# Split fp32r projections in the first mixer, one modulation moved to TensorE, dummy matmuls in the routing, and nineteen weight chunks loaded ahead

## The chip, the cores and the metric

One NeuronCore of a Trainium2 chip runs the whole kernel. The time is that of the device for one execution, in microseconds (us); the time shown for a kernel is the median of its runs. The profile is of one further execution, with its own time. The engines are TensorE (PE, matrix products), VectorE (DVE), ScalarE (ACT), GpSimd (POOL) and SyncE (SP), which here issues the transfers of the weights. PEld is TensorE's loading of the stationary operand. The granted clock of TensorE is given as a share of its full 2.4 GHz.

## The reference

A trunk of two layers over 256 tokens of width 1024. Each layer normalizes, scales and shifts its input by columns that are computed from a conditioning vector c (six modulations per layer: shift, scale and gate of the mixer, shift, scale and gate of the feed-forward part), runs a mixer, adds its gated output, and does the same with a feed-forward part. The part of the reference that the change touches:

```python
# layer 0, mixer: one input projection split into u, v (A) and p (B)
u, v = split(gelu(uv));  v = layernorm(v)
sv = einsum('gts,bnsgd->bntgd', tril(w_s), v) + b_s        # chunks of 128 tokens
a  = u * sv
pooled = trailing_mean(p, windows 2, 4, 8, 16) - p
b  = einsum('bsgd,gde->bsge', pooled, w_grp) * scale
x  = x + gate * (concat(a, b) @ w_out)

# layer 1, feed-forward: top 2 of 8 experts
logits = h @ router_w
top_v, top_i = top_k(logits, 2);  wts = softmax(top_v)
y = sum_e gates[..., e] * swiglu(h, w_gu[e], w_down[e])    # 8 experts, 1024 -> 3584 -> 1024
```

The ada modulations are `c_act @ ada_w + ada_b`, a matrix of 1024 x 6144 per layer. All weights are float32 in device memory, 466 MB that are read once.

## The kernel before, in words

The kernel streams the weights in chunks of 1 MB (128 partitions x 2048 float32) from SP's queue into a ring of buffers named `raw`: 5 at first, 8 more (`keep`) and 3 more (`extra`) when the dense part has ended. A list `order` says which chunk comes next; whenever a buffer is left (`leave`) the next load is issued.

Products of the dense part are made of fp32r matmuls: an operand x is split into a rounded part H and the remainder L, and x w is taken as xH wH + xL wH + xH wL, three matmuls. ACT makes H (line 121), DVE subtracts to get L (line 124). The first mixer is an exception: its projection of `vp` (v and p, line 649) and its `gate_u` (line 666) multiply in plain float32, where one matmul is executed as several passes and shows two records.

The first mixer: `normed` gives the normalized tokens; the class `HT` transposes them in quarters q = 0 to 3 on PE (`flip`, line 285) and evacuates each quarter with its scale and shift (`evac`, line 299 on DVE). The scale and shift of a quarter come from `ada(0, 1, q)` and `ada(0, 0, q)`, each two weighted sums over a chunk on DVE (line 568) and a bias (line 596). A modulation can be computed on PE instead, with `ada_rows`: 16 small row products (line 579), a copy of the row by ACT (line 585), and `turn`: four products with one column (line 589) and the bias on DVE (line 591). The loop over q runs in an order written out by hand: within `tc.manual_schedule` the instructions of an engine are kept in the order of the program text. What stands behind the closing of that order (`hand.close()`) is placed by a planner, which orders by estimated times, until the next hand-written part. After the loop come `gate_u(0)`, the gelu of v, its layernorm on DVE and POOL (lines 683 to 691), the pooling matrices (lines 704 to 713), `gate_u(1)`, the products with w_s (line 730), and the output projection with split operands (lines 316 to 322 and 356 to 359), followed by the flips and the feed-forward part of layer 0 from 106 us.

The routing of layer 1: `Close` finishes the residual of layer 1's mixer, the tokens are flipped (line 1300) and multiplied with the router (line 1314), `Route.top2` finds the two experts of each token (lines 427 to 436), `place` and `counts` count the tokens of each expert with small products (lines 441 to 449). An expert's tokens are collected with a 0/1 matrix P, which `Gather.rows` builds by comparing slots with a row of integers (`iota`, line 1388; Q on line 1390), and `pick64` multiplies with the tokens (line 1416); `part64` evacuates. Then `seq`, a list of chunk events, is run: per block four chunks of gate/up weights and two of down weights. Experts with up to 64 tokens (S) use plain float32 with the two halves of the array's columns (lines 1527 and 1547), experts with up to 128 (L) use the split. S and L blocks alternate with LEAD = 3 blocks of S ahead; FIRST = 16 is the number of chunks before the first L block, and up to so many chunks are loaded, as far as buffers are free (16), before the first event runs. The last expert ends with `scatter2_front` (line 1553) and the addition into the result.

## Time and profile before

| what | value |
|---|---|
| median of 3 runs | 1250.69 us (1250.29 to 1253.85) |
| profiled execution | 1250.61 us |
| its span, first to last instruction | 1248.6 us |
| mean granted clock of TensorE | 0.989 |
| PE / DVE / ACT / POOL busy | 1199.2 / 735.3 / 501.3 / 67.7 us |
| read from device memory | 465.76 MB, 374 GB/s over the span |

Share of the span by engine and by stage are read from different views: the page sums over everything, while windows of a few us show which engine is full in one stage. A busy PE is one with a matmul in flight; at half clock it is as busy as at full clock. A gap of PE has beside it the instruction that released it, in brackets in the timeline. Records of matmuls overlap, so their pitch is read from the starts.

### The profile page before, as it was taken

To read this page: it belongs to the slowest core of one execution; us is meant where nothing else is said; L and a number is where in the kernel's file an instruction comes from. 1 tells how busy PE (TensorE), PEld (TensorE's weight loads), DVE (VectorE), ACT (ScalarE), POOL (GpSimd) and SP (SyncE) were. 2 spreads that over 40 slices of the span, in tenths; PEclk is the share of its full clock that TensorE was granted. 3 is DMA by queue.
4 is the path that set the end of the run, shared out by engine and by line. 5 is a ranking of instruction groups with operands and counts; after the bars stand their busy time and mean duration, and the time that the engine had idled before them with its cause. 6 is when DMAs were issued, how large, how long until landed. Compare 5 with 4: busy or idle time off the path is not lost.

```text
span 1248.6 us, 18665 instructions
## 1 busy us (share of the span) xinstructions
PE 1199.2 (96%) x7255; PEld 866.1 (69%) x7255; DVE 735.3 (59%) x1098; ACT 501.3 (40%) x775; POOL 67.7 (5%) x105
## 2 busy tenths in 40 slices
PE   5999999999999899999999999999999999999997
PEld 2577999997987666666666676666675666666663
DVE  5797988886895355546264656263555652653531
ACT  2147443445763234444153344252433541433410
POOL 2810000001320000000000000000000000000000
PEclk9999999999999799999999999999999999999999
DMA  9898999984657899999999999999999999999995
GB/s 357 352 376 306 354 337 349 355 313 176 237 203 277 343 405 421 419 419 419 419 420 419 419 420 419 420 419 420 419 419 412 418 419 420 420 420 418 420 418 202
DMA packets 65904, 468.11 MB, mean 375 GB/s; under 512 B 7568, under 2 KB 7824, under 8 KB 9616
## 3 DMA queue, kind: packets, MB, share of 16 engines
q1 hardware_dynamic: 65520, 466.32, 92.5%
q8 instruction: 59, 0.97, 0.3%
q10 hardware_dynamic: 288, 0.52, 0.1%
q14 instruction: 37, 0.30, 0.1%
HBM read 465.76 MB, written 1.05 MB: 374 GB/s over the span
## 4 chain that ended last, share of the span: by engine, by line
PE 85%; DVE 7%; issue 2%; ACT 2%; POOL 1%; DMA 1%; SPq 0%; DVEq 0%; ACTq 0%; POOLq 0%
PE gu L1527 20%; PE o L1547 10%; PE o L316 3%; PE g L316 3%; PE pb L337 3%; PE g L318 3%; PE u L318 3%; PE o L318 3%; PE u L316 3%; PE o L322 3%; PE g L322 3%; PE pb L335 3%; PE u L322 3%; PE pb L334 3%; PE pa L649 2%
## 5 line engine op out<-in xcount | busy, mean ns | idle before, releaser
L121 ACT CAST H<-raw 128x1024 fp32r<-128x1024 f32 x350 | 344.2, 1047 | 34.2 <-PE pb L335 13.2
L147 DVE TENSOR_TENSOR raw<-raw,H 128x1024 fp32r<-128x1024 f32 x252 | 297.5, 1222 | 39.9 <-ACT H L121 22.6
L1527 PE MATMUL gu<-raw,hgS 128*64 128x256 f32 x2240 | 253.8, 383 | 0.0
L1527 PEld LDWEIGHTS gu<-raw,hgS 128*64 128x64 f32 x2240 | 157.4, 137 | 89.0 <-issue 13.8
L124 DVE TENSOR_TENSOR L<-raw,H 128x1024 fp32r<-128x1024 f32 (+1 forms) x98 | 118.2, 1219 | 26.6 <-PE pb L337 14.5
L1547 PE MATMUL o<-raw,aS 128*64 128x512 f32 x560 | 130.4, 599 | 0.0
L568 DVE SCALAR_TENSOR_TENSOR junk<-raw,cact 128x1024 bf16<-128x1024 f32 x88 | 108.8, 1259 | 8.4 <-DMA raw<-in_ada 8.2
L334 PE MATMUL pb<-hH,H 128*128 128x256 f32 x432 | 103.1, 279 | 0.0
L335 PE MATMUL pb<-hL,H 128*128 128x256 f32 x432 | 102.9, 279 | 0.0
L1533 DVE TENSOR_TENSOR msg<-msg,gu 128x256 f32<-128x256 f32 x35 | 14.7, 421 | 125.2 <-ACT msg L1532 125.1
L1547 PEld LDWEIGHTS o<-raw,aS 128*64 128x64 f32 x560 | 37.0, 137 | 64.3 <-issue 60.0
L334 PEld LDWEIGHTS pb<-hH,H 128*128 128x128 f32 x432 | 81.2, 188 | 0.4
L335 PEld LDWEIGHTS pb<-hL,H 128*128 128x128 f32 x432 | 81.1, 188 | 0.4
L1481 DVE TENSOR_TENSOR msg<-msg,u 128x512 f32<-128x512 f32 x21 | 14.4, 687 | 109.0 <-ACT msg L1480 109.0
L1532 ACT ACTIVATE msg<-gu 128x256 f32<-128x256 f32 x35 | 13.4, 384 | 161.3 <-PE gu L1527 161.2
L1480 ACT ACTIVATE msg<-g 128x512 f32<-128x512 f32 x21 | 12.5, 597 | 151.3 <-PE g L322 151.3
L316 PE MATMUL g<-H,hgH 128*128 128x512 f32 x168 | 67.3, 401 | 0.0
L322 PE MATMUL u<-raw,hgH 128*128 128x512 f32 x168 | 66.5, 396 | 0.0
L318 PE MATMUL g<-H,hgL 128*128 128x512 f32 x168 | 66.5, 396 | 0.0
L318 PE MATMUL u<-H,hgL 128*128 128x512 f32 x168 | 66.4, 395 | 0.0
L316 PE MATMUL u<-H,hgH 128*128 128x512 f32 x168 | 66.3, 395 | 0.0
L322 PE MATMUL g<-raw,hgH 128*128 128x512 f32 x168 | 66.3, 394 | 0.0
(391 smaller groups left out, 1631.4 us busy)
## 6 DMA issues: line engine op xcount, KB each, us to landing
raw<-in_mgu SPq DMA_DIRECT2D x224, 1024.0 KB, 16.0
raw<-in_mdn SPq DMA_DIRECT2D x112, 1024.0 KB, 15.3
raw<-in_ada SPq DMA_DIRECT2D x48, 1024.0 KB, 6.9
raw<-in_fgu SPq DMA_DIRECT2D x22, 1024.0 KB, 7.7
raw<-in_fdn SPq DMA_DIRECT2D x11, 1024.0 KB, 7.5
raw<-in_oin_c SPq DMA_DIRECT2D x6, 1024.0 KB, 5.3
raw<-in_ein_vp SPq DMA_DIRECT2D x4, 1024.0 KB, 9.3
raw<-in_eout SPq DMA_DIRECT2D x4, 1024.0 KB, 7.2
```

Of the source, the lines that this page charges most:

```text
L121: act.copy(self.to(q), raw[:, q * self.f:(q + 1) * self.f])
L124: eng.tensor_tensor(self.to(q), raw[:, q * self.f:(q + 1) * self.f], high.half(q).bitcast(F32), OP.subtract)
L147: vec.tensor_tensor(l[:, at], raw[:, at], h.half(q).bitcast(F32), OP.subtract)
L316: pe.matmul(o, xH(k, i), wH(k, n), start=first and m == 0, stop=False)
L318: pe.matmul(o, xL(k, i), wH(k, n), start=False, stop=False)
L322: pe.matmul(o, xH(k, i), wL(k, n), start=False, stop=last and m == len(ks) - 1)
L334: pe.matmul(o, wH(k), hH[:, k, :], start=(k == 0), stop=False)
L335: pe.matmul(o, wH(k), hL[:, k, :], start=False, stop=False)
L337: pe.matmul(o, wL(k), hH[:, k, :], start=False, stop=(k == KD - 1))
L568: vec.scalar_tensor_tensor(junk, raw[:, a * D:(a + 1) * D], 1.0, cact, OP.mult, OP.mult, accum_out=mods[:, l, j + a:j + a + 1])
L1527: pe.matmul(gu[HALF[h], n * 256:(n + 1) * 256], g_.full[:, k, :], w[:, lo:lo + 256], start=(k == 0 and n == 0), stop=(k == KD - 1), skip_g ...
L1547: pe.matmul(o[HALF[h]], a[:, kk, c, :], w[:, kk * D + h * 512:kk * D + (h + 1) * 512], start=(j == 0 and c == 0 and kk == 0), stop=(j == 6 ...
```

## The change

In the first mixer, the loop over the quarters is rewritten. The transposed tokens are split (H and L). The chunk of weights is split as well, and each quarter's product is three fp32r matmuls, 12 for each of the quarter's two rows of 128 (`vp_part`). `gate_u` uses the split product too. The shift's modulation `ada(0, 0, q)` moves from DVE to PE (`ada_rows` and `turn`), with its weights laid out in another order of the same bytes. In the routing, `warm(n)` issues n products of bf16 ones of 512 columns into a PSUM tile that nobody reads; it is called five times. POOL's second row of integers is removed, and `rows` compares with a repeated view of the first. `scatter2_front` multiplies once over 128 partitions with a row that ACT has copied beforehand. LEAD becomes 4 (FIRST is then 22), and the loads before the first event are issued in another order: chunks 3 to 15 into 13 free buffers, then chunks 0 to 2 as `Plain`, each by two transfers into two of the six half buffers in which the rounded parts of the dense stage lay, then chunks 16 to 18.

```diff
--- before.py
+++ after.py
@@ -25,6 +25,7 @@
 CH = 2048
 RING = 5
 RING2, RING3 = 8, 3
+EARLY = 13
 HB, LB = 6, 5
 NJ = DFF // 128
 
@@ -597,7 +598,7 @@
 
     BD = [(0, 512), (512, 1024)]
 
-    with Phase("mix0", w8=5, w4=5, w2=6) as pool:
+    with Phase("mix0", w8=6, w4=5, w2=6) as pool:
         sm = pool
         lrow = pool.tile([128, 2048], F32, tag="w8", name="lrow")
         bands = pool.tile([128, 4, 3, 128], F32, tag="w8", name="bands")
@@ -631,23 +632,32 @@
         hand = ctx.enter_context(ExitStack())
         hand.enter_context(tc.manual_schedule(engines=MAN | {mybir.EngineType.Pool}))
         xn = normed()
-        ht = HT(pool, xn, 0, False, split_it=False)
-        h0 = ht.full
+        ht = HT(pool, xn, 0, False)
+        h0H, h0L = ht.H, ht.L
         vp = [[psa() for _ in range(2)] for _ in range(2)]
+
+        def vp_part(q, ks, w):
+            mm3_b([[vp[part][i] for part in range(2)] for i in range(2)], ks, toks(h0H), toks(h0L),
+                  wcols(w[0], q * 2, D, BD), wcols(w[1], q * 2, D, BD), ks[0] == 0, ks[-1] == KD - 1)
+
         ht.flip(0)
+        ada(0, 1, 0)
+        turn = ada_rows(0, 0, 0)
         for q in range(4):
+            turn()
+            ht.evac(q)
+            raw, _ = raw_of("vp", q)
+            w = high_part(raw, CH), Halves("L", LB, CH)
+            ht.low(q, vec)
+            for half in range(2):
+                w[1].less(half, raw, w[0])
             if q < 3:
                 ht.flip(q + 1)
-            ada(0, 1, q)
-            ada(0, 0, q)
-            ht.evac(q)
-            w, _ = raw_of("vp", q)
-            for kk in range(2):
-                k = q * 2 + kk
-                for part in range(2):
-                    for i in range(2):
-                        pe.matmul(vp[part][i], h0[:, k, i * 128:(i + 1) * 128],
-                                  w[:, kk * D + part * 512:kk * D + (part + 1) * 512], start=(k == 0), stop=(k == 7))
+                ada(0, 1, q + 1)
+            vp_part(q, (q * 2,), w)
+            if q < 3:
+                turn = ada_rows(0, 0, q + 1)
+            vp_part(q, (q * 2 + 1,), w)
             if q == 1:
                 mean_bands()
         hand.close()
@@ -658,12 +668,11 @@
         uT = pool.tile([128, 4, S], F32, tag="w4", name="uT")
 
         def gate_u(c):
-            w, _ = raw_of("u", c)
+            w = split_of("u", c)
             ps = psb()
             for cc in range(2):
-                for k in range(KD):
-                    o = k * 256 + cc * 128
-                    pe.matmul(ps[:, cc * 256:(cc + 1) * 256], w[:, o:o + 128], h0[:, k, :], start=(k == 0), stop=(k == 7))
+                mm3_a(ps[:, cc * 256:(cc + 1) * 256], *(lambda k, t=t: t[:, k * 256 + cc * 128:k * 256 + cc * 128 + 128] for t in w),
+                      h0H, h0L)
             return ps
 
         gu_ps = gate_u(0)
@@ -1314,6 +1323,15 @@
                 pe.matmul(lgp[i][:, :NE], t[:, q, :], aR[:, k, :], start=(k == 0), stop=(k == KD - 1))
 
         cl_ = Close(pool, outs, [out_part(c, wo[c]) for c in (2, 3)], grow)
+        idle = []
+
+        def warm(n):
+
+            if not idle:
+                idle.append(psa("idle"))
+            for _ in range(n):
+                pe.matmul(idle[0], onesb, onesb[:, None, :].to_broadcast([128, 4, 128]), start=True, stop=True)
+
         route = Route(lgp, cl_.ss)
         keep = ctx.enter_context(Phase("keep", side="right", **{f"raw{n}": 1 for n in range(RING2)}))
         free[2:2] = [(keep, f"raw{n}") for n in range(RING2)]
@@ -1343,8 +1361,10 @@
         route.top2(0)
         use(1, 0)
         route.place(0)
+        warm(8)
         cl_.add(1, 1)
         flip(1, 1)
+        warm(3)
         cl_.square(1, 1)
         cl_.rstd(1)
         use(1, 1)
@@ -1358,11 +1378,9 @@
     shcol = mods[:, 1, 24:32]
     with Phase("experts", w4=1, w2=2, aTL=1, hgH=1, hgL=1, hgS=1, P=1, Q=1, PT=4) as pool:
         sm = pool
-        iota2 = pool.tile([128, 128], F32, name="iota2")
+
+        pool.tile([128, S], F32, tag="PT", name="PT")
         ranks, caps = pool.tile([128, NE], F32, name="ranks"), pool.tile([128, 2 * NE], F32, name="caps")
-        for half in range(2):
-            gp.iota(iota2[:, half * 64:half * 64 + 64], pattern=[[1, 64]], base=0, channel_multiplier=0,
-                    allow_small_or_imprecise_dtypes=True)
         for n in range(NE):
             gp.memset(ranks[:, n:n + 1], float(RANKS[n]))
             for s_ in range(2):
@@ -1385,7 +1403,9 @@
                 self.got = {}
 
             def rows(self, i):
-                vec.tensor_scalar(self.P[:, i, :], iota if self.cap == 128 else iota2,
+                w = self.cap
+                vec.tensor_scalar(self.P[:, i, :].rearrange("p (n w) -> p n w", w=w),
+                                  iota[:, None, :w].to_broadcast([128, 128 // w, w]),
                                   self.slots[0][i], self.slots[1][i], op0=OP.is_equal, op1=OP.mult)
                 vec.tensor_scalar(self.Q[:, i, :self.cap], self.P[:, i, :self.cap], cl_.ss[i][:, 3:4], None, op0=OP.mult)
 
@@ -1549,8 +1569,7 @@
 
         def scatter2_front(o):
             og = sm.tile([128, 512], F32, tag="w2", name=nm("og"))
-            for h in range(2):
-                vec.tensor_tensor(og[HALF[h]], o[HALF[h]], grow[HALF[h], h * 512:(h + 1) * 512], OP.mult)
+            vec.tensor_tensor(og, o, grow2, OP.mult)
             return og
 
         def scatter2_back(gcol, og, g_, last=False):
@@ -1587,7 +1606,7 @@
 
         streams = {k: [(k, p, j) for p in range(NE) if (CAPS[p] == 128) == (k == "L") for j in range(7)] for k in "SL"}
         blocks, nS, nL = [], len(streams["S"]), len(streams["L"])
-        LEAD = 3
+        LEAD = 4
         for n in range(nL):
             while len(blocks) - n < LEAD + (nS - LEAD - 2) * n // nL:
                 blocks.append(streams["S"][len(blocks) - n])
@@ -1656,7 +1675,8 @@
                 if (j, c) == (0, 0):
                     outs_[p] = psa("o")
                 down2_chunk(outs_[p], j, c, acts[p, j], chunk)
-            leave(chunk[1] if kind[0] == "L" else chunk)
+            if not isinstance(chunk, Plain):
+                leave(chunk[1] if kind[0] == "L" else chunk)
             if kind[1] == "U" and c == 3:
                 close_up(kind, p, j)
             if kind[1] == "D" and c == 1 and j == 6:
@@ -1708,21 +1728,37 @@
                 after(2, lambda: scatter2_back(w_.gcol, og, w_.g))
 
 
+        grow2 = pool.tile([128, 512], F32, name="grow2")
         cur = Gather(slots_of(stat, 0), 64, 4)
         cur.rows(0)
+        warm(2)
         cur.pick64(0)
         route.top2(1)
+        warm(5)
         route.place(1)
         cur.rows(1)
         route.counts()
+        warm(5)
         cur.pick64(1)
         cur.part64()
         work[0] = Work(0, stat)
         work[0].g = cur
-
-        for n in range(min(len(free), FIRST)):
-            chunks[seq[n]] = load(weights(*seq[n]), CH)
-            loaded[0] += 1
+        class Plain:
+
+
+            def __init__(self, src):
+                self.h = Halves("H", HB, CH)
+                for q in range(2):
+                    sp.dma_start(self.h.to(q).bitcast(F32), src[:, q * D:(q + 1) * D])
+
+            def __getitem__(self, at):
+                return self.h[at].bitcast(F32)
+
+
+        first = HB // 2
+        loaded[0] = min(len(free) + first, FIRST)
+        for n in [*range(first, first + EARLY), *range(first), *range(first + EARLY, loaded[0])]:
+            chunks[seq[n]] = Plain(weights(*seq[n])) if n < first else load(weights(*seq[n]), CH)
         for n, ev in enumerate(seq):
             run(ev)
             if n == 0:
@@ -1732,6 +1768,8 @@
                 grows = [gate_row(1, 5, m, psb()) for m in range(2)]
             if n == 2:
                 grow = gate_copy(pool, grows)
+                for h in range(2):
+                    act.copy(grow2[HALF[h]], grow[HALF[h], h * 512:(h + 1) * 512])
             if n == FIRST - 5:
                 gather_steps(1)
             part(n + AHEAD)
@@ -1804,7 +1842,7 @@
     uq = np.concatenate([uq[:, :, :128].reshape(256, 512), uq[:, :, 128:].reshape(256, 256)], axis=1)
     ada = I["ada_w"].transpose(0, 2, 1).reshape(2, 6, 4, 2, 128, 1024).transpose(0, 1, 2, 4, 3, 5).copy()
     by_d = I["ada_w"][0].reshape(8, 128, 6, 4, 256).transpose(2, 3, 1, 0, 4).reshape(6, 4, 128, 2, 1024)
-    ada[0, 3:5, 2:4] = by_d[3:5, 2:4]
+    ada[0, 3:5, 2:4], ada[0, 0] = by_d[3:5, 2:4], by_d[0]
     arrays = {
         "x": I["x"][0], "c": I["c"], "pos": I["positions"][0].reshape(2, 128).T,
         "cols": cols, "rows": rows,
```

## Rows read from the trace of the kernel before

**Rows 1.** Page, part 1: busy time of each engine, share of the span, instructions

```profile
PE 1199.2 (96%) x7255; PEld 866.1 (69%) x7255; DVE 735.3 (59%) x1098; ACT 501.3 (40%) x775; POOL 67.7 (5%) x105
```

**Rows 2.** Waits of PE, 425 to 1249 us: total, times, longest

```profile
PE pt L1398 <- DVE Q L1390: 3.6, 2, 1.8
```

**Rows 3.** Windows: busy time by engine (columns PE, PEld, DVE, ACT, POOL), clock, DMA share, GB/s

```profile
1232.00:1234.00 2.00, 2.00 (x12) 0.68 (x10) 0.00 (x0) 0.00 (x0) 0.00 (x0) 1.00 0.04 16
```

**Rows 4.** Timeline of PE, vp and gate_u: start, us, line, tiles, count, idle before

```profile
17.04 9.94 PE L649 MATMUL pa<-raw,hF 128*128 128x512 f32 x16 [3.49 <-DVE hF L299]
...
44.62 7.13 PE L649 MATMUL pa<-raw,hF 128*128 128x512 f32 x16 [1.09 <-DVE hF L299]
51.59 7.07 PE L666 MATMUL pb<-hF,raw 128*128 128x256 f32 x32
...
69.89 1.05 PE L730 MATMUL pt<-wsT,v 128*128 128x128 f32 x8
```

**Rows 5.** Timeline of PE, mixer's products and the turns

```profile
76.41 2.00 PE L322 MATMUL pa<-L,catH 128*128 128x512 f32 x8
78.24 0.63 PE L316 MATMUL pa<-H,catH 128*128 128x512 f32 x2
...
94.44 1.07 PE L579 MATMUL pb<-raw,ccol 128*32 128x256 f32 x16
...
103.96 0.61 PE L589 MATMUL pb<-quart,row 128*128 128x1 f32 x4
...
114.33 1.12 PE L839 MATMUL pa<-hH,L 128*128 128x256 f32 x8
```

**Rows 6.** Timeline of DVE: a turn's bias and an evacuation

```profile
104.67 0.16 DVE L591 TENSOR_TENSOR mods<-pb,cols 128x2 f32<-128x2 f32 x1 [1.77 <-PE pb L589]
...
106.03 0.99 DVE L299 TENSOR_SCALAR hf<-pt,acol,mods 128x256 f32<-128x256 f32 x2
```

**Rows 7.** Timeline of ACT: the rounded copy of an evacuated quarter

```profile
105.98 0.62 ACT L301 CAST hH<-hf 128x512 fp32r<-128x512 f32 x1
```

**Rows 8.** Page, part 5: groups by line, busy us and mean ns of one, idle before

```profile
L121 ACT CAST H<-raw 128x1024 fp32r<-128x1024 f32 x350 | 344.2, 1047 | 34.2 <-PE pb L335 13.2
...
L124 DVE TENSOR_TENSOR L<-raw,H 128x1024 fp32r<-128x1024 f32 (+1 forms) x98 | 118.2, 1219 | 26.6 <-PE pb L337 14.5
```

**Rows 9.** Windows, 50 to 100 us

```profile
50.00:100.00 50.00, 48.26 (x257) 38.45 (x256) 45.08 (x73) 20.49 (x34) 16.85 (x10) 1.00 0.87 338
```

**Rows 10.** Timeline of PE, routing, and an expert's gather

```profile
406.44 0.63 PE L1300 MATMUL pt<-ident,x 128*128 128x128 f32 x4 [1.67 <-DVE x L366]
...
410.91 3.64 PE L1416 MATMUL pt<-Q,x 128*128 128x64 f32 x16 [1.78 <-DVE lg L427]
...
419.12 3.39 PE L1527 MATMUL gu<-raw,hgS 128*64 128x256 f32 x16
...
425.70 5.40 PE L1527 MATMUL gu<-raw,hgS 128*64 128x256 f32 x48
...
670.59 3.71 PE L1398 MATMUL pt<-Q,x 128*128 128x128 f32 x16 [1.84 <-DVE Q L1390]
```

**Rows 11.** Windows, routing and the first chunks

```profile
408.00:412.00 4.00, 2.22 (x14) 2.16 (x13) 2.32 (x10) 0.37 (x2) 1.67 (x27) 0.55 1.02 422
...
420.00:424.00 4.00, 4.00 (x28) 2.22 (x26) 3.25 (x19) 0.58 (x2) 0.00 (x0) 0.74 0.10 39
424.00:428.00 4.00, 4.00 (x38) 2.65 (x36) 1.18 (x6) 2.36 (x3) 0.00 (x0) 1.00 0.89 289
```

**Rows 12.** Timeline of DVE, the routing's P, and the last og

```profile
409.63 0.84 DVE L1388 TENSOR_SCALAR P<-iota,stat 128x128 f32<-128x128 f32 x1 [1.07 <-POOL iota L1364]
...
414.82 0.34 DVE L1388 TENSOR_SCALAR P<-iota,stat 128x128 f32<-128x128 f32 x1
...
1237.97 1.41 DVE L1553 TENSOR_TENSOR og<-o,grow 64x512 f32<-64x512 f32 x2 [7.56 <-PE o L1547]
```

**Rows 13.** DMA view, 423 to 424.5 us: issues, KB each, us to landing

```profile
raw<-in_mgu SPq DMA_DIRECT2D x1, 1024.0 KB, 4.7
```

## The prediction, made before the changed kernel was built or run

> **What bounds the kernel now.** I read the page first. TensorE (PE) is busy for 96% of the span [rows 1], so the kernel is bound by PE unless PE waits for data. In the expert stage it does not: from 425 us to the end the waits of PE name VectorE and ScalarE, the longest group being 3.6 us, and never a transfer [rows 2]. The stream of weights stays only a little ahead, though. It still moves 16 GB/s in 1232 to 1234 us, which is the last of it [rows 3], while the span ends at 1248.6. So whatever moves the start of the expert stage moves the end, as long as the stream moves with it. Two stretches before it are touched: the first mixer (15 to 100 us) and the routing (404 to 428 us). The profiled execution took 1250.61 us for a span of 1248.6; I add to that time, which lies within 0.1 us of the median of the runs, 1250.69.
>
> **First mixer, price of the matmuls.** Before, one quarter q of the vp projection is 8 plain f32 matmuls of 512 columns, 7.1 us in the quarter at 44.62 [rows 4]. After, it is 24 fp32r matmuls. Eight such run from 76.41 to the start of the next at 78.24 [rows 5], so the pitch is 0.23 us and a quarter costs 24 x 0.23 = 5.6 us. To it come 16 row products (1.07) and 4 tiny products, the turn (0.61, of which 0.5 until PE goes on), for the shift's modulation [rows 5]. With the four transposes, 0.47 in both kernels, PE has the same work as before: 5.6 + 1.0 + 0.5 = 7.1.
>
> **First mixer, the order.** What changes is the waiting. Before, the evacuation of quarter q depends on DVE's own modulations, and PE works on quarter q-1 meanwhile. After, the turn of quarter q stands on PE behind all 24 matmuls of quarter q-1, and the first matmul of quarter q needs this chain: the turn until its bias on DVE starts (0.71 us, the distance of L589 at 103.96 from L591 at 104.67 [rows 5, 6]), 0.2 for the scale column, 0.99 for the two halves of the evacuation [rows 6], 0.62 for the rounded copy on ACT [rows 7], then the first cast of the weights, 1.05 [rows 8], which stands behind that copy on ACT; with 0.3 for handovers, 3.85 us. PE fills 0.5 of it with the turn and 0.47 with the next transposes, so it idles 2.9 us per quarter, and the period is 5.6 + 1.0 + 3.85 = 10.45 us. Before, the three periods from 17.04 to 44.62 were 9.2 on average, the first of them slow: its 16 records took 9.94 instead of 7.1 [rows 4]. The first matmul moves from 17.04 to about 18.7 (copy and cast). Then 3 x 10.45, 2.9 for the slow first quarter and 5.6 for the last give 18.7 + 31.4 + 2.9 + 5.6 = 58.6, against 51.7: **+6.9 us**. If the first quarter is not slow this time, +4.0.
>
> **First mixer, what comes back.** The two gate_u products cost 48 x 0.114 = 5.5 us each (8 of 256 columns in 1.12 with the last one's tail [rows 5], which is half the pitch of 512 columns) instead of 6.9 (7.07 with its tail [rows 4]): -2.8 for the two. PE idles 1.7 of the 50 us from 50 to 100 [rows 9]; a later start can swallow that. If PE alone decides, the mixer's products end 6.9 - 2.8 - 1.7 = +2.4 later. DVE decides otherwise: it is busy 45.1 of those 50 us [rows 9], gets four more subtractions of 1.22 for u [rows 8], 4.9 us, and loses nothing there, since the modulation that leaves it was done before 50 us; in its place come two such subtractions per quarter. With all of its 4.9 idle us used up it ends +6.9 later, and with a third of them not to be used +8.5. I take the middle of 2.4 and 6.9, 4.6, and 0.4 for some matmuls at half clock: **+5.0 us**. Bounds: -0.5 (4.0 - 2.8 - 1.7) to +10.4 (8.5 and one loss of clock, 1.9, from the next paragraph).
>
> The price of a half clock comes from an expert's gather. After 1.84 us of idle PE, 16 records took 3.71 us at 670.59 [rows 10], as in the routing's gather at half clock (3.64 [rows 10]); at full clock it would be half, so one loss is 1.9 us. Not every wait brings it: the quarter at 44.62 had a wait of 1.09 before it and ran in 7.13 [rows 4]. No row here shows three waits of 2.9 us close together, so what they do to the clock is open: nothing, or up to 3 x 1.9 = 5.7 us. The Trainium skill, "TensorE: Matmul & The Clock Gate", section "Why this matters for your kernels", advises against leaving TensorE idle between bursts of matmuls, because it falls back to the lower clock. The wait of 1.84 before the slow gather agrees with that, the one of 1.09 before a full-speed quarter shows that it needs more than a short one.
>
> **Routing.** The granted clock is 0.55 in 408 to 412 us and 0.74 in 420 to 424 [rows 11], after PE waits such as the 1.67 us at 406.44 [rows 10]. Three edits act here. First, P at 409.63 waited 1.07 for POOL's iota and took 0.84 beside POOL's fills against 0.34 at 414.82 [rows 12]: -1.5 on the chain to pick64. Second, the dummy matmuls (23, 0.23 each at full clock by the 512-column pitch) fill the waits: the 8 cost 1.8 in the wait of 1.67, the 3 cost 0.7 in a shorter one behind it; the twelve afterwards stand in the wait of 1.78 [rows 10] and before the second pick, where they can push by 0.3 to 0.6. At full clock pick64 takes 1.83 instead of 3.64 and the first chunk 1.8 (the 48 matmuls at 425.70 took 5.40) instead of 3.39 [rows 10]. Walking the order: pick64(0) at 409.3, the chain of place(1) done at 412.8, pick64(1) from 413 to 414.9, part64 1.0, first chunk 415.8 (before: 419.12), third chunk from 421.0 (before: 425.70): -4.7, with the spread of the pushes up to -4.9.
>
> Third, the loads. A single chunk into an idle queue lands 4.7 us after its issue [rows 13], and in the full stream, 422 GB/s [rows 11], one takes 2.49, so use starts some 2.2 us after the last byte. The sixteen chunks of before end at 420.4 (39 GB/s x 4 us of 420 to 424 is 0.16 MB, 0.4 us of stream [rows 11]). After, thirteen go first and end at 412.9; chunks 0, 1 and 2 follow and are usable at 417.6, 420.1 and 422.6. The third chunk's last matmuls then end at 423.5, against 425.70 + 1.8 = 427.5 before: **-3.9 us**, the landing rather than PE being last. If the chunks come sooner, -4.9. The Plain halves issue six DMAs for three; they stand in a full queue and cost no time by themselves. The three chunks more keep the stream busy where it ran at 39 and 289 GB/s in 420 to 428 [rows 11], 3.6 + 1.3 = 4.9 us of stream time, so it ends earlier by that relative to PE, and the slack behind 1234 us grows. LEAD 4 shifts which block follows which, with the same instructions; its worth is one half-clock loss either way at a gather, 0 +- 1.9.
>
> **End.** og is two operations of 64 partitions in 1.41 us on the last chain, at 1237.97 [rows 12]; as one of 128 it is 0.7: **-0.7**. The two copies into grow2 on ACT lie beside PE's chunks: nothing.
>
> **Sum.** +5.0 - 3.9 - 0.7 = +0.4: **1251.0 us**.
>
> **Rivals.** (A) The mixer costs nothing: the first quarter runs at full rate, PE decides, -0.5; routing -4.9, end -0.7: 1250.6 - 6.1 = **1244.5**. For it: PE's idle 1.7 us can be used, and u is cheaper. Against it: DVE at 90% [rows 9]. (B) Slower: the turn behind the matmuls. From the point where DVE rather than PE delivers the eo weights' low parts, its extra 4.9 us count whole, +8.5, and one half-clock loss, +1.9, in vp: 10.4 - 3.9 - 0.7 = +5.8, **1256.4**. For it: PE already waits at a quarter for DVE's hF [rows 4]. Against it: DVE has some 3 us per quarter free (10.45 less four operations of 1.22, the evacuation, and 1.4 of small ones), into which the later ada steps could be placed. (C) Each of the three waits of 2.9 us in vp drops the clock: 5.7 in place of the 0.4 that I took, +5.7, **1256.3**. For it: half that wait sufficed before the gather at 670.59. Against it: the rest of a quarter is dense. (D) The dummies don't hold the clock: the twelve of the second half at 0.46 add 5.5 us, the wait of 1.78 and the iota's 1.5 give back 3.3, so routing is +2.2 instead of -3.9: 1250.6 + 5.0 + 2.2 - 0.7 = **1257.1**. Against it: they have 512 columns each and stand back to back in the very waits after which the clock fell.
>
> **How the numbers follow.** Forecast 0.44, A 0.27, B 0.13, C 0.06, D 0.10. A measurement tells 0.3% from no change, 3.75 us: faster is below 1246.9, slower above 1254.4. The forecast's own range is 1247 to 1254; A lies below it, B, C and D above. So faster 0.27, same 0.44, slower 0.29, and the range that leaves out 2 in 10 goes from 1244.3 to 1258.0.
>
> **What would show it.** In the changed trace vp should end near 58.6, with waits of PE for ACT's casts of 2 to 3 us before each quarter; L730's products should start 3 to 4 us later than 69.89, and the eo products end near 103. The clock should be 1.00 from 404 to 428, the first chunk start at 416 to 418 and wait for its DMA, the third end near 423.5 plus the mixer's delay. If vp ends before 55 or the dense stages close the gap, it goes to A; if PE waits for L124 after the mixer's products begin, to B; if the clock falls to 0.5 in the quarters, to C; if it stays there in 412 to 416, to D.

## The result, and the profile after

The changed kernel is slower: 1262.9 us (median of 6 runs, 1258.4 to 1267.8) against 1251.1 in the same series; the ratio is 1.0095, 95% interval 1.0078 to 1.0113. Its runs lie 9 us apart, those of before 4 us. The profiled execution is the quickest of the six, 1258.35 us with a span of 1256.5. So the trace shows 7.7 of the 11.8 us; the rest lies in executions without a trace, in which the mean granted clock was 0.983 to 0.987 instead of 0.990. Span times one less the clock gives an estimate of what the lower clock took: 12.6 us in the quickest run, 21.5 in the slowest (span 1266.0 us, clock 0.983). The difference of 8.9 is nearly all of the 9.4 us between the two, so by this estimate the scatter comes from the clock.

Four points in the two traces divide the loss (start of the instruction, us):

| point | before | after | difference |
|---|---|---|---|
| second row product behind the mixer's output projection (L579 / L580) | 98.42 | 108.96 | +10.5 |
| first count of the routing, `place(0)` (L441 / L442) | 404.60 | 415.22 | +10.6 |
| third chunk of the experts (L1527 / L1547) | 425.70 | 431.89 | +6.2 |
| last block of down weights (L1547 / L1567) | 1230.83 | 1238.31 | +7.5 |

The first mixer loses 10.5, the dense stages hand it on, the routing returns 4.4 and the experts lose 1.3 again.

PE's timeline of the changed kernel in the first mixer (start, us, line, operation, tiles, count, idle before and its releaser) answers to [rows 4]:

```profile
31.83 0.73 PE L317 MATMUL pa<-H,hH 128*128 128x512 f32 x2 [2.52 <-ACT H L122]
...
42.24 0.73 PE L317 MATMUL pa<-H,hH 128*128 128x512 f32 x2 [2.52 <-ACT H L122]
...
53.03 0.74 PE L317 MATMUL pa<-H,hH 128*128 128x512 f32 x2 [3.41 <-ACT H L122]
...
59.34 1.08 PE L323 MATMUL pa<-L,hH 128*128 128x512 f32 x4
...
76.29 0.46 PE L739 MATMUL pt<-wsT,v 128*128 128x128 f32 x2 [0.16 <-ACT ybT L725]
81.02 3.03 PE L739 MATMUL pt<-wsT,v 128*128 128x128 f32 x14 [4.26 <-POOL v L700]
```

The waits before the quarters are there, 2.5, 2.5 and 3.4 us for ACT's cast, and vp ends at 60.4, 8.7 us later than before. But a second wait, 4.3 us, stands where before had none: the products with w_s wait for POOL. POOL's chain over v, first in the kernel before, from its first to its last operation:

```profile
51.75 1.61 POOL L688 TENSOR_TENSOR lrs<-lrs,nhalf 128x1 f32<-128x1 f32 x1 [3.00 <-DVE lrs L687]
...
65.06 1.60 POOL L691 TENSOR_TENSOR v<-v,lrow 128x512 f32<-128x512 f32 x1
```

and in the changed kernel, with one of the middle:

```profile
64.90 1.55 POOL L697 TENSOR_TENSOR lrs<-lrs,nhalf 128x1 f32<-128x1 f32 x1 [15.54 <-DVE mv L694]
66.56 3.67 POOL L698 TENSOR_SCALAR v<-v,mv,lrs 128x512 f32<-128x512 f32 x1
...
79.70 1.26 POOL L700 TENSOR_TENSOR v<-v,lrow 128x512 f32<-128x512 f32 x1
```

It started at 51.75 and ended at 66.7, 3.2 us before PE wanted it at 69.89 [rows 4]; now it starts at 64.9 and ends at 80.96, and PE stands ready at 76.8. The 14 products behind the wait take 3.03 us where 8 took 1.05 before [rows 4], and the granted clock is 0.68 in 80 to 84 us and 0.90 in 84 to 88, some 1.7 us lost. Later the mixer gets 1.9 us back: the kernel before had two waits of PE for L124 in the output projection, 1.03 us at 87.32 and 0.64 at 88.46, and the changed kernel has none. So the 10.5 us are, each rounded, 8.7 of vp, -2.3 up to the products with w_s (76.29 against 69.89, gate_u being shorter), 6.1 of the wait for POOL with the half clock behind it, and -1.9.

Two things delay the start of POOL's chain by 13 us, more than vp's 8.7. ACT's gelu of v reads two PSUM tiles that before were complete while the p columns of the last quarter were still being multiplied; the first gelu and the first statistics of the kernel before:

```profile
49.22 0.60 ACT L673 ACTIVATE v<-pa 128x512 f32<-128x512 f32 x1 [35.97 <-PE pa L649]
49.85 0.69 DVE L683 BATCH_NORM_STATS2 bn<-v 128x6 f32<-128x512 f32 x1 [4.83 <-ACT v L673]
```

Now all four tiles end together, and the gelu is 10.6 us later:

```profile
59.77 1.09 ACT L682 ACTIVATE v<-pa 128x512 f32<-128x512 f32 x2 [2.65 <-PE pa L323]
```

And the statistics of v then wait on DVE behind operations that the planner put ahead of them, weighted sums of modulations (L569) and the subtraction for u's new low part (L125). They are 12.4 us later, and a further weighted sum behind them makes it 13.15 at POOL:

```profile
58.78 1.22 DVE L569 SCALAR_TENSOR_TENSOR junk<-raw,cact 128x1024 bf16<-128x1024 f32 x1
...
61.07 1.22 DVE L125 TENSOR_TENSOR L<-raw,H 128x1024 fp32r<-128x1024 f32 x1
...
62.28 1.28 DVE L692 BATCH_NORM_STATS2 bn<-v 128x6 f32<-128x512 f32 x2
```

The routing after, on PE, answers to the routing rows of [rows 10]:

```profile
415.25 1.89 PE L1333 MATMUL idle<-onesb 128*128 128x512 bf16 x8
...
419.87 1.97 PE L1436 MATMUL pt<-Q,x 128*128 128x64 f32 x16
...
425.81 1.95 PE L1547 MATMUL gu<-H,hgS 128*64 128x256 f32 x16
...
428.53 1.08 PE L1547 MATMUL gu<-H,hgS 128*64 128x256 f32 x8 [0.40 <-DMA H<-in_mgu]
429.85 1.08 PE L1547 MATMUL gu<-H,hgS 128*64 128x256 f32 x8 [0.24 <-DMA H<-in_mgu]
...
431.89 1.95 PE L1547 MATMUL gu<-H,hgS 128*64 128x256 f32 x16
```

and two of its windows (columns as in [rows 3]) answer to [rows 11]:

```profile
420.00:424.00 4.00, 4.00 (x31) 2.77 (x32) 2.94 (x18) 0.00 (x0) 0.65 (x20) 1.00 1.02 417
424.00:428.00 4.00, 4.00 (x35) 3.00 (x34) 1.84 (x10) 1.29 (x4) 0.00 (x0) 1.00 1.00 401
```

The clock is 1.00 throughout, against 0.74 in the first of these stretches before, pick64 takes 1.97 instead of 3.64, the second chunk waits for its two half transfers, and the stream doesn't pause: 417 and 401 GB/s against 39 and 289. From 425 us on PE's waits (total, times, longest) answer to [rows 2]. The group of the `y` additions, first in the kernel before:

```profile
PE pt L1560 <- DVE y L1454: 3.0, 4, 0.8
```

and the changed kernel's list:

```profile
PE pt L1579 <- DVE y L1474: 4.8, 4, 1.8
PE pt L1418 <- DVE Q L1410: 3.6, 2, 1.8
...
PE gu L1547 <- DMA H<-in_mgu: 0.6, 2, 0.4
```

The `y` group has grown from 3.0 us to 4.8, its longest wait from 0.8 to 1.8. Last, og, which answers to the last row of [rows 12], and behind it PE's first product with it, of the changed kernel:

```profile
1245.45 0.69 DVE L1572 TENSOR_TENSOR og<-o,grow 128x512 f32<-128x512 f32 x1 [7.56 <-PE o L1567]
```

```profile
1246.19 1.13 PE L1579 MATMUL pt<-og,PT 64*128 64x512 f32 x4 [0.79 <-DVE og L1572]
```

The same product of the kernel before:

```profile
1238.71 1.48 PE L1560 MATMUL pt<-og,PT 64*128 64x512 f32 x3 [0.79 <-DVE og L1553]
```

Og is half as long, but PE started 0.74 us behind its start in both: before, the first half of 64 partitions was enough to start with. So the shorter og brought nothing.

### The profile page after: what moved, and what is told of

Same layout as the page of the kernel before. It is cut to its first block, busy times and chain, and to the rows that moved or that the text cites. A ratio compares the mean times of both kernels' runs of the same rounds, so it can differ in the third digit from the quotient of the medians.

```text
span 1256.5 us, 19038 instructions
## 1 busy us (share of the span) xinstructions
PE 1201.2 (96%) x7422; PEld 876.9 (70%) x7422; DVE 735.6 (59%) x1093; ACT 516.6 (41%) x797; POOL 69.3 (6%) x103
## 3 DMA queue, kind: packets, MB, share of 16 engines
HBM read 465.76 MB, written 1.05 MB: 372 GB/s over the span
## 5 line engine op out<-in xcount | busy, mean ns | idle before, releaser
L122 ACT CAST H<-raw 128x1024 fp32r<-128x1024 f32 x362 | 356.1, 1047 | 32.1 <-DMA raw<-in_fdn 8.7
L1547 PE MATMUL gu<-raw,hgS 128*64 128x256 f32 x2192 | 245.8, 381 | 0.0
L1547 PEld LDWEIGHTS gu<-raw,hgS 128*64 128x64 f32 x2192 | 154.0, 137 | 85.1 <-issue 11.2
L125 DVE TENSOR_TENSOR L<-raw,H 128x1024 fp32r<-128x1024 f32 (+1 forms) x110 | 134.0, 1233 | 28.2 <-PE pb L338 13.7
L1567 PE MATMUL o<-raw,aS 128*64 128x512 f32 x560 | 130.2, 599 | 0.0
L335 PE MATMUL pb<-hH,H 128*128 128x256 f32 x464 | 110.8, 279 | 0.0
L336 PE MATMUL pb<-hL,H 128*128 128x256 f32 x464 | 110.5, 279 | 0.0
L569 DVE SCALAR_TENSOR_TENSOR junk<-raw,cact 128x1024 bf16<-128x1024 f32 x80 | 97.2, 1235 | 1.5 <-DMA raw<-in_ada 1.5
L335 PEld LDWEIGHTS pb<-hH,H 128*128 128x128 f32 x464 | 87.2, 188 | 0.5
L336 PEld LDWEIGHTS pb<-hL,H 128*128 128x128 f32 x464 | 87.1, 188 | 0.4
L1567 PEld LDWEIGHTS o<-raw,aS 128*64 128x64 f32 x560 | 36.9, 136 | 64.2 <-issue 58.7
L1500 ACT ACTIVATE msg<-g 128x512 f32<-128x512 f32 x21 | 12.5, 597 | 157.0 <-PE g L323 157.0
```

The costliest lines, as they stand in the source:

```text
L122: act.copy(self.to(q), raw[:, q * self.f:(q + 1) * self.f])
L125: eng.tensor_tensor(self.to(q), raw[:, q * self.f:(q + 1) * self.f], high.half(q).bitcast(F32), OP.subtract)
L335: pe.matmul(o, wH(k), hH[:, k, :], start=(k == 0), stop=False)
L336: pe.matmul(o, wH(k), hL[:, k, :], start=False, stop=False)
L569: vec.scalar_tensor_tensor(junk, raw[:, a * D:(a + 1) * D], 1.0, cact, OP.mult, OP.mult, accum_out=mods[:, l, j + a:j + a + 1])
L1547: pe.matmul(gu[HALF[h], n * 256:(n + 1) * 256], g_.full[:, k, :], w[:, lo:lo + 256], start=(k == 0 and n == 0), stop=(k == KD - 1), skip_g ...
```

## The experiments

Intervals are of the ratio to the kernel before, run on the same chip in the same series. The median of before was 1251.2 us in the series of experiments 1 to 4, 1250.4 in that of 5, 6, 7 and 11, and 1251.4 in that of 8, 9, 10 and 12. So kernels of different series are compared by their differences from before.

**1. The old mixer with everything else changed.** Here and below, the edit stands as a short diff against the changed kernel.

```diff
-    with Phase("mix0", w8=6, w4=5, w2=6) as pool:
-        ht = HT(pool, xn, 0, False)
...
+    with Phase("mix0", w8=5, w4=5, w2=6) as pool:
+        ht = HT(pool, xn, 0, False, split_it=False)
...
-            w = split_of("u", c)
+            w, _ = raw_of("u", c)
```

> The changed kernel with the first mixer of before; everything from the routing on as changed. Theory M (the whole loss is made in the first mixer, 10.6 us in the profiled run and more in others through the clock; the routing gives 4 back): 1246 to 1249 us, runs within 4 us of each other as before, the third chunk of the experts about 4.4 us earlier than in the kernel before. Rival E (part of the loss and the scatter of the runs come from the reordered experts with LEAD 4): 1251 us or more, and runs 5 to 10 us apart.

Measured: 1252.9 us (10 runs, 1249.1 to 1255.2), ratio 1.0011 (0.9996 to 1.0025). The mixer makes most of the loss, 10 us, but the routing's gain does not arrive: theory M missed by 4 us and rival E held. From `place(0)` to the third chunk it took 16.5 us against 21.1 before. What took the gain away lies behind that.

**2. Only the mixer changed.** The edit is the mixer's part of the diff on the kernel before.

```diff
-                pe.matmul(ps[:, cc * 256:(cc + 1) * 256], w[:, o:o + 128], h0[:, k, :], start=(k == 0), stop=(k == 7))
+                mm3_a(ps[:, cc * 256:(cc + 1) * 256], *(lambda k, t=t: t[:, k * 256 + cc * 128:k * 256 + cc * 128 + 128] for t in w),
+                      h0H, h0L)
...
```

> The kernel before with only the first mixer changed. Theory M: 1262 to 1270 us, wide apart, products of the mixer done 10 to 11 us later than before. Rival E: 1255 to 1259 us, and close together.

Measured: 1266.1 us (4 runs, 1262.4 to 1268.3), ratio 1.0117 (1.0093 to 1.0142), as M said. In the profiled execution, 1268.3 us, the second row product behind the output projection stands at 115.20, 16.8 us late, where M said 10 to 11. The mixer's code is that of the changed kernel, whose profiled execution has the point at 108.96. What is added is clock: 0.79 in 32 to 40 us, 0.79 in 44 to 52 and 0.57 in 56 to 64, behind the waits before the second, third and fourth quarter, and 0.57 in 84 to 92 behind the wait for POOL. The trace of experiment 8, again with the same mixer, has the half clock behind all three quarters' waits, vp and POOL's chain 2.6 us later than in the changed kernel, and the point at 111.60.

**3. The shift's modulation back on DVE.**

```diff
-            turn()
             ht.evac(q)
...
                 ada(0, 1, q + 1)
+                ada(0, 0, q + 1)
```

> The changed kernel with the shift's modulation back on DVE, vp still in fp32r. Theory T (the turn behind the 24 matmuls makes the wait before each quarter): the wait moves from PE's turn to DVE, which has 9.2 us per quarter (two modulations 5.0, two subtractions 2.45, low half 0.7, evacuation 1.0), so the period falls from 10.4 to about 9.7, vp ends 2 to 3 us earlier, 1258 to 1261 us. Rival S (the split itself, casts and subtractions, makes the wait): the same as the changed kernel, 1262 to 1264 us.

Measured: 1261.6 us (4 runs, 1257.9 to 1265.3), ratio 1.0085 (1.0054 to 1.0115). It lies at the edge of both: PE's waits before the quarters stayed, at 2.1, 3.4 and 3.6 us for ACT's cast, so moving the modulation alone does not remove them. Inconclusive on T, whose 1258 to 1261 holds one of the four runs. The periods in its trace, 10.4, 11.2 and 11.0 us, are not the 9.7 of T, and half clock follows each of the three waits.

**4. The turn early.**

```diff
                 ht.flip(q + 1)
                 ada(0, 1, q + 1)
+                turn = ada_rows(0, 0, q + 1)
             vp_part(q, (q * 2,), w)
             if q < 3:
-                turn = ada_rows(0, 0, q + 1)
+                turn()
+                ht.evac(q + 1)
             vp_part(q, (q * 2 + 1,), w)
```

> The changed kernel with the row products ahead of a quarter's first half and the turn and evacuation of the next quarter between its two halves. Theory T: the waits of 2.5 to 3.4 us before the quarters go, period 7.6 to 8.5 us, vp ends at 51 to 54 instead of 60.2, the time is 1251 to 1255 us with the wait for POOL's chain over v left. Rival S: the period stays above 9.5 and the time above 1259 us.

Measured: 1258.1 us (4 runs, 1256.3 to 1259.4), ratio 1.0067 (1.0050 to 1.0084). The waits of 2.5 to 3.4 us for the casts went, but the row products, now earlier, waited 3.05, 1.44 and 1.18 us for the transfer of their weights, and the first quarter began at 23.4 instead of 19.8. The periods were 10.2, 8.9 and 6.8 us, and the time fell by 5 us and not by 8 to 12, between the two ranges. PE's timeline of this kernel, the end of vp and the products with w_s:

```profile
54.25 1.09 PE L323 MATMUL pa<-L,hH 128*128 128x512 f32 x4
...
77.10 1.65 PE L741 MATMUL pt<-wsT,v 128*128 128x128 f32 x6 [5.65 <-POOL v L702]
```

vp ended at 55.3, 5 us earlier than in the changed kernel, but the wait for POOL grew to 5.65 us: the statistics of v ran on DVE at 59.28, some 3.5 us after v was there, behind four weighted sums. The quarters' order was one limit, POOL's chain the next.

**5. Dummy products in the three waits.**

```diff
+            if q:
+                fill = psb("fill")
+                for _ in range(FILL[q]):
+                    pe.matmul(fill, fillb, fillb[:, None, :].to_broadcast([128, 4, 128]), start=True, stop=True)
             vp_part(q, (q * 2,), w)
```

> The changed kernel with 11, 11 and 15 dummy products of 512 columns in the waits before the second, third and fourth quarter of vp. They add nothing to the result and fill the waits of 2.5, 2.5 and 3.4 us. Theory C (part of the loss, and the scatter of the runs, is a half clock after these waits): no half clock between 20 and 62 us, 1258 to 1261 us. Rival W (the waits alone are the loss): 1262 to 1264 us as the changed kernel.

Measured: 1262.6 us (4 runs, 1258.4 to 1264.8), ratio 1.0107 (1.0085 to 1.0129). In this kernel's window over vp the clock is full and PE is busy for 41.56 of 42 us:

```profile
20.00:62.00 42.00, 41.56 (x232) 28.98 (x231) 30.57 (x51) 15.82 (x22) 21.23 (x27) 1.00 0.85 336
```

v was evacuated at 57.86 instead of 59.77, yet the statistics and POOL's chain began where they did, at 61.93 and 64.56:

```profile
61.93 1.28 DVE L699 BATCH_NORM_STATS2 bn<-v 128x6 f32<-128x512 f32 x2
```

```profile
64.56 1.54 POOL L704 TENSOR_TENSOR lrs<-lrs,nhalf 128x1 f32<-128x1 f32 x1 [15.56 <-DVE mv L701]
```

So the half clock in the last quarter cost PE 1.9 us in the changed kernel's trace, and none of it reached the end, because DVE's order held v. The time is in W's range, for a reason that neither theory named. This says nothing of half clock in the earlier quarters, which the changed kernel's trace doesn't have and those of experiments 2 and 8 do; there it moved the whole mixer. The runs still lie 6 us apart: in this trace half clock stands behind the wait for POOL, now 6.3 us long, and behind one of the additions (experiment 7).

**6. LEAD 3 with the old mixer.** The edit is on the kernel of experiment 1.

```diff
-        LEAD = 4
+        LEAD = 3
```

> The changed kernel with the first mixer of before and LEAD 3. The kernel with the old mixer and LEAD 4 did not keep the 4 us that the routing gains, and its trace has two waits of 2.4 us at the addition of an expert where before has 1.4, with a half clock behind each. Theory L (the block order of LEAD 4 loses what the routing gains): 1245.5 to 1247.5 us, the waits back at 1.4 us, no half clock there. Rival P (the gain of the routing is lost by something else, as the stream of weights): 1250 to 1252 us.

Measured: 1246.1 us (9 runs, 1243.8 to 1250.1), ratio 0.9969 (0.9954 to 0.9983), faster than before. Theory L held: the longest wait at an addition is 0.84 us again, with full clock behind it.

**7. LEAD 4 alone on the kernel before.** The edit is the reverse.

```diff
-        LEAD = 3
+        LEAD = 4
```

> The kernel before with LEAD 4 alone. Theory L: 1253 to 1258 us, two waits of 2.4 us in the experts instead of 1.4, in most runs with a half clock behind. Rival P: 1250 to 1252 us.

Measured: 1256.9 us (4 runs, 1256.0 to 1260.8), ratio 1.0053 (1.0034 to 1.0072). One line costs 6.5 us. Why is seen at the addition of the first expert that ends. PE's timeline of the kernel before at that addition:

```profile
576.39 1.78 PE L1560 MATMUL pt<-og,PT 64*128 64x512 f32 x4 [0.84 <-DVE y L1454]
```

and with LEAD 4 alone:

```profile
572.36 1.90 PE L1560 MATMUL pt<-og,PT 64*128 64x512 f32 x4
576.25 2.73 PE L1560 MATMUL pt<-og,PT 64*128 64x512 f32 x4 [1.99 <-DVE y L1454]
```

and a window of this kernel behind it:

```profile
577.00:581.00 4.00, 4.00 (x8) 2.11 (x8) 2.73 (x4) 0.00 (x0) 0.00 (x0) 0.50 1.01 420
```

The second half of the products waits until DVE has added the first half, because both PSUM tiles (`pst` has two) are taken. What DVE does meanwhile, in the same trace:

```profile
571.62 1.40 DVE L1553 TENSOR_TENSOR og<-o,grow 64x512 f32<-64x512 f32 x2
573.05 2.36 DVE L147 TENSOR_TENSOR raw<-raw,H 128x1024 fp32r<-128x1024 f32 x2
575.45 1.41 DVE L1454 SCALAR_TENSOR_TENSOR y<-pt,stat,x 128x512 f32<-128x512 f32 x2
```

With LEAD 4 the addition falls beside a block of an L expert, and two subtractions for its weights (L147, 2.36 us) stand on DVE between og and the addition. In the kernel before DVE was idle there and waited for PE. The wait doubles from 0.84 to 2.0 us, and this happens at two additions, the second at 764.72; the clock is 0.83 over the 20 us from 572 and over those from 760, which gives an estimate of 3.4 us lost at each. With the longer waits that is more than the 6.5 us of the median: the execution with the trace is the slowest of the four.

The half clock does not always follow. In the changed kernel's trace the same wait is 1.8 us and the clock behind it is full:

```profile
579.95 1.78 PE L1579 MATMUL pt<-og,PT 64*128 64x512 f32 x4 [1.79 <-DVE y L1474]
```

```profile
580.00:605.00 25.00, 25.00 (x140) 16.09 (x141) 12.81 (x14) 7.44 (x10) 0.00 (x0) 1.00 1.01 419
```

Behind waits of the same 1.8 us the four products took 2.73 us instead of 1.78 at both additions in experiment 1, and 2.55 at one of the two in experiment 5. So LEAD 4 costs the waits in each of these traces and the clock in some, which makes it one likely source of the scatter. (The 1.4 and 2.4 us of the expectations are the distances from the start of the last product before the wait to that of the first behind it.)

**8. LEAD 3 alone in the changed kernel.** The edit is that of 6, on the whole change.

```diff
-        LEAD = 4
+        LEAD = 3
```

> The changed kernel with LEAD 3 alone. If the parts add up: the block order of LEAD 4 cost 6.9 us with the old mixer and 6.5 with everything old, so 1262.9 - 6.7: 1255 to 1257.5 us, and the additions' two waits of 2.4 us back at 1.4. If the mixer's loss already covers it: 1261 to 1263.

Measured: 1259.0 us (6 runs, 1256.6 to 1260.0), ratio 1.0065 (1.0051 to 1.0079): 7.7 us above before where the changed kernel is 11.8 above it, so 4.2 us less and not 6.7, though its group of waits for the addition is back at 3.0 us. The direction is that of adding parts, the size is between the two; the changed kernel's own scatter of 9 us is larger than the gap.

**9. Without the dummy products of the routing** (old mixer, LEAD 3).

```diff
-            for _ in range(n):
+            for _ in range(0):
```

> The kernel with the old mixer and LEAD 3, without the 23 dummy products in the routing. Theory K (they hold the clock): half clock for 10 to 14 us in the routing again, the third chunk 2 to 4 us later, 1248 to 1250 us. Rival N (the loads and the integers did it): 1245.5 to 1247 us.

Measured: 1251.0 us (10 runs, 1247.9 to 1254.5), ratio 0.9997 (0.9985 to 1.0008), against 0.9969 with them: 4.0 us more, as differences from before. PE's timeline and a window of this kernel:

```profile
410.77 3.65 PE L1428 MATMUL pt<-Q,x 128*128 128x64 f32 x16 [0.23 <-DVE Q L1402]
...
426.34 1.95 PE L1539 MATMUL gu<-H,hgS 128*64 128x256 f32 x16
```

```profile
420.00:424.00 4.00, 4.00 (x22) 1.89 (x20) 3.25 (x18) 0.58 (x2) 0.00 (x0) 0.54 0.06 23
```

pick64 takes 3.65 again and from `place(0)` to the third chunk it is 20.2 us, against 17.0 with them and 21.1 before. Theory K held, with a time 1 us above its range; the dummies carry 3.2 of the 4.1 us to the third chunk, and the time without them is that of before.

**10. Sixteen chunks in their order** (old mixer, LEAD 3).

```diff
-        first = HB // 2
+        first = 0
-        for n in [*range(first, first + EARLY), *range(first), *range(first + EARLY, loaded[0])]:
+        for n in range(loaded[0]):
```

> The kernel with the old mixer and LEAD 3, with sixteen chunks loaded ahead in their order as before. PE starts the experts up to 1 us earlier, as nothing waits for the three chunks that came last. Theory S (the stream must have the three chunks more, or it falls behind the faster start): the last chunks come late, waits for a transfer in the experts, 1248 to 1250 us. Rival N (the preload is hidden): 1245 to 1246.5 us.

Measured: 1244.0 us (4 runs, 1242.2 to 1245.3), ratio 0.9943 (0.9926 to 0.9960), the fastest of all, 3.0 us less than with nineteen (experiment 6) as differences from before. With nineteen ahead the second chunk waits for its transfer and the third starts 17.0 us after `place(0)`; PE's timeline of that kernel (experiment 6):

```profile
417.98 1.08 PE L1539 MATMUL gu<-H,hgS 128*64 128x256 f32 x8 [0.77 <-DMA H<-in_mgu]
...
421.31 1.95 PE L1539 MATMUL gu<-H,hgS 128*64 128x256 f32 x16
```

and of this one, where it starts after 15.7:

```profile
418.40 1.95 PE L1539 MATMUL gu<-raw,hgS 128*64 128x256 f32 x16
...
421.29 5.40 PE L1539 MATMUL gu<-raw,hgS 128*64 128x256 f32 x48
```

The stream does not fall behind: it dips to 334 GB/s in this kernel's window, where with nineteen ahead it dips to 279 in 416 to 420 us and 341 in 420 to 424, and no wait of PE for a transfer appears from 404 us on:

```profile
420.00:424.00 4.00, 4.00 (x38) 2.69 (x36) 2.08 (x11) 2.99 (x5) 0.00 (x0) 1.00 0.94 334
```

Theory S failed, and the time is 1 us below N's range: the preload is hidden, and loading the first three chunks last costs 1.3 us up to the third chunk. Where the rest of the 3.0 us lies was not followed.

**11. v first** (turn early, LEAD 3).

```diff
+            if q == 3:
+                for part in range(2):
+                    mm3_b([[vp[part][i]] for i in range(2)], (6, 7), toks(h0H), toks(h0L),
+                          wcols(w[0], 6, D, BD[part:]), wcols(w[1], 6, D, BD[part:]), False, True)
+                continue
...
+            vec.bn_stats(st, v)
```

> The turn early as in the kernel of that name, the last quarter of vp one half of the columns after the other so that v is done first, the statistics of v by hand ahead of DVE's other work, and LEAD 3. Theory V (after the quarters the mixer waits for POOL's chain over v, which starts late): the chain starts at 54 to 56 instead of 62, the wait of 5.9 us before the products with w_s falls below 1, and the time is 1244 to 1248 us. Rival D (DVE's eight more subtractions hold the output projection anyway): a new wait for L before the output projection's products, 1249 to 1253 us.

Measured: 1250.5 us (12 runs, 1248.5 to 1253.3), ratio 1.0006 (0.9995 to 1.0017), above V's range. The time is in D's range, but not for D's reason: PE never waits for L in the output projection. The chain starts at 57.9 and not at 54 to 56, since weighted sums still stood between the statistics on DVE. It takes 17.5 us from its first operation to its last, against 14.9 in the kernel before, and PE still waits 3.4 us:

```profile
58.57 4.04 POOL L707 TENSOR_SCALAR v<-v,mv,lrs 128x512 f32<-128x512 f32 x1
...
74.14 1.26 POOL L709 TENSOR_TENSOR v<-v,lrow 128x512 f32<-128x512 f32 x1
```

**12. The three operations on v on DVE** (v first, LEAD 3).

```diff
-            gp.tensor_scalar(v, v, mv[:, 0:1], r, op0=OP.subtract, op1=OP.mult)
-            gp.tensor_tensor(v, v, lrow[:, R_LW:R_LW + 512], OP.mult)
-            gp.tensor_tensor(v, v, lrow[:, R_LB:R_LB + 512], OP.add)
+            vec.tensor_scalar(v, v, mv[:, 0:1], r, op0=OP.subtract, op1=OP.mult)
+            vec.tensor_tensor(v, v, lrow[:, R_LW:R_LW + 512], OP.mult)
+            vec.tensor_tensor(v, v, lrow[:, R_LB:R_LB + 512], OP.add)
```

> The kernel with v first and LEAD 3, the three operations on each half of v on DVE instead of POOL. Theory V (POOL's chain over v is what the new mixer still waits for): v is done by 64 to 66 us instead of 75.4, the wait of 3.4 us before the products with w_s goes, 1245 to 1248 us. Rival D (DVE's four operations more per half push the low parts of the output projection): 1249 to 1252 us with waits of PE for L.

Measured: 1247.6 us (12 runs, 1245.2 to 1250.8), ratio 0.9973 (0.9962 to 0.9984). DVE's first and last operation on v, and PE's remaining products with w_s, in this kernel:

```profile
60.36 0.51 DVE L707 TENSOR_SCALAR v<-v,mv,lrs 128x512 f32<-128x512 f32 x1
...
64.86 0.69 DVE L709 TENSOR_TENSOR v<-v,lrow 128x512 f32<-128x512 f32 x1
```

```profile
72.44 1.27 PE L748 MATMUL pt<-wsT,v 128*128 128x128 f32 x10
```

v is done at 65.6 and PE does not wait for it. Theory V held: with the quarters unbound and POOL's three operations out of the path, the new mixer costs 0.6 us more than the old one of experiment 6 (ratios 0.9973 and 0.9969, intervals overlapping) instead of 12. It is still no gain: in the traces its second row product stands at 101.93, against 98.24 in experiment 6.

## Why the prediction was wrong

The forecast was 1251.0 us, with a range from 1244.3 to 1258.0; 1262.9 us were measured.

**The bound and the way of the loss through the dense stages: right.** The 10.5 us of the mixer stand unchanged at `place(0)`, and no wait for a transfer appears behind 435 us.

**The price of the matmuls and the wait before each quarter: right.** The first quarter began at 19.8 instead of 18.7. The three periods are 12.0, 10.4 and 10.8 us, against 13.35 (10.45 and 2.9 for the slow first quarter) and twice 10.45; vp ended at 60.4 against 58.6, with 1.9 us lost to half clock in its last quarter. The waits are 2.5, 2.5 and 3.4 us where 2.9 was worked out.

**What comes back in the mixer: the step that failed.** It asked whether PE or DVE would decide, and set +2.4 and +6.9 against each other. POOL decided, a path that the step does not name. The two paybacks that it counted did come: 2.3 us up to the products with w_s for gate_u's 2.8, and 1.9 in the output projection for PE's idle 1.7. But the chain from v over ACT, DVE and POOL to the products with w_s runs beside gate_u, so what gate_u saved became waiting. POOL's part takes 14.9 us from its first operation to its last before and 16.1 after, and its slack was 3.2 us, less than half of vp's delay. The +8.7 of vp, 1.9 for the later end of v's tiles and 2.6 in DVE's queue made +13.15 at POOL's first operation; with 1.15 more in POOL's operations and the slack taken off, the products with w_s begin 11.1 us late (81.02 against 69.89). The half clock behind that wait makes it 12.5 in the output projection, and 10.5 are left when PE's two waits there are gone. Experiments 4, 11 and 12 show the cause: with the waits for the casts gone the wait for POOL grew, with v ahead in DVE's queue it fell to 3.4 us, and with POOL's operations on DVE it went. The mixer's term is +5.0 in the sum; it measures +10.5 in the trace and +12.0 in medians (experiments 8 and 6). The upper bound of 10.4 was given to PE waiting for DVE's low parts, which did not occur; DVE's queue counted in another place, ahead of v's statistics.

**Half clock in the quarters (rival C): not in the profiled execution, but in others.** The changed kernel's trace has one such loss in vp, which did not reach the end (experiment 5). The traces of experiments 2 and 8, with the same mixer, have it behind all three waits, as C said, and there the mixer ended 6.2 and 2.6 us later. How much of the changed kernel's median this makes stays open, as its slower executions have no trace and filling the waits did not lower the median.

**Routing: right in size, and in mechanism but for the loads.** -3.9 to the third chunk was forecast, -4.4 measured, the clock full, the dummies worth 4.0 us in medians (experiment 9). Only the second chunk waited for its transfer; the step had the third one's landing as the last. What it credited to the nineteen chunks was not there: sixteen do better by 3 us (experiment 10).

**LEAD 4 at 0 +- 1.9: the second failure.** It measures +6.5 alone (experiment 7), by the order of DVE's work around the additions and the half clock behind them. The step called it the same instructions in another order and did not ask what stands on DVE between og and the addition.

**The end at -0.7: wrong**, for PE was released by og's first half already.

In medians, each as its difference from before in its own series: the mixer +12.0 (experiment 8 against 6), LEAD 4 +4.2 (the changed kernel against 8), the rest -4.3 (experiment 6). They add up to the measured +11.8 by construction, so the sum is no check of the parts. LEAD 4 costs 6.5 us alone, 6.1 with the old mixer and 4.2 with the new one. That the half clock behind the additions comes in some executions and not in others can make such differences; that it made these is not shown.

## What to carry to other kernels

When a stage is delayed, follow each chain that leaves it, on every engine, to its own consumer, and write down its slack; work that PE saves beside a chain does not shorten the chain. When the order of blocks changes, look at what an in-order engine will run between two halves of a short exchange with PE: two DVE operations of 1.2 us each there cost 1 us of waiting and, in some executions, the clock behind it. Dummy matmuls in the short waits of the routing were worth 4 us, while in the waits of the mixer, where another engine's chain set the end, they were worth nothing; and a preload that the stream hid cost time. One trace of a kernel whose runs scatter is one of several cases: the mean clock of the other runs tells whether it is the mild one.

## What the runs showed of the hardware that was not expected

A wait of 2.0 us at an addition was followed by a granted clock of 0.50 (experiment 7), one of 0.84 at the same point by none in the kernel before, whose clock was 1.00 there. Waits of 1.8 us at this point were followed by half clock in experiment 1 and by full clock in the changed kernel. The same mixer ended 10.5, 13.2 and 16.8 us late in three traces (the changed kernel, experiments 8 and 2), with half clock behind one, three and three of its quarters' waits. POOL's subtraction and scaling of 128x512 of v took 2.08 to 4.14 us in these kernels, DVE's 0.51 to 0.55 (experiment 12).
